# Attention with the values as weights, transposed outputs, and scores from 64-row products of two heads in turn

## The chip, the cores and the metric

The kernel runs on one core of a Trainium2 chip. The core has a matrix engine (TensorE, PE in the profile), which multiplies a stationary operand (the weights, up to 128 rows by 128 columns) with a moving one (up to 512 columns) and writes to PSUM; VectorE (DVE), ScalarE (ACT) and GpSimd (POOL), which work elementwise; SyncE (SP), from whose queue nearly all DMA transfers start; and 16 DMA engines. The metric is the device time of one execution in microseconds (us). Three runs of the kernel before took 1360.21, 1360.32 and 1365.02 us, median 1360.32.

## The reference, cut to what matters

One layer of a hybrid decoder with 1024 tokens of width 1024, in float32: a norm and one projection, then an attention group (8 heads of 64) beside an RWKV-7 group, an output projection with a norm and a residual, and a feed-forward block. The change is in the attention and in the output projection behind it:

```python
A = causal LongNet-style dilated sliding-window attention, branches (128,1),(512,4),(2048,16),
    branch outputs combined by their softmax denominators; then RMSNorm over the attention group
...
attn = _rms_norm(_dilated_attention(q, k, v), attn_out_gain[i])
mixed = jnp.concatenate([attn, rw], axis=-1) @ w_out[i]
x = x + _rms_norm(mixed, norm_mix_post[i])
```

All three branches together are one softmax over all keys up to the query, in which a key counts as often as branches reach it. The kernel therefore adds one strip of constants to the scores (`stripT`, the logarithm of that count, or a very large number where no branch reaches) and does one softmax for each query.

## The kernel before

**Order of the work.** The norm, the projections and the RWKV-7 group come first (lines 194 to 819); there an explicit order for PE and SP is written out. Three projections of the last head pair (`z_aq`, `z_ak`, `z_av`, of which the last two remain) are left over as `rest` and run beside the attention. Then come four calls of `attn_pair(p)` (line 837), one for each pair of heads, at a raised priority, with loads of output weights (`load_wo`, line 923) in between. From there to the end of the attention the order on each engine is chosen when the program is built: a list scheduler takes, by priority and by its own estimate of times, what is ready. Each engine then executes its own list in that order, waiting on semaphores where needed.

**One head pair.** Queries and keys lie in DRAM (`zs_d`) with channels on the partitions: 128 rows, two heads of 64. For each head the query is loaded twice, into both halves of the partitions; the upper half becomes the rounded value (type fp32r, which TensorE multiplies in one pass) and the lower half the remainder, so that one product over 128 rows multiplies both parts of the query with the rounded key (`kh`, also twice) and a second one with the key's remainder (`kl`): two products for each head, `mm` in line 888. Scores have 128 queries on the partitions and up to 1024 keys in the columns, in one or two banks of PSUM (`pS`, tag `w`, two banks). For query block i (0 to 7), both heads: VectorE adds the strip and finds the minimum (line 890; the query is scaled by -0.125, so the largest score is the minimum), ScalarE takes the exponential with its sum in `den` (line 893), PE transposes up to eight blocks of 128 (line 900), and ScalarE (first four) and VectorE (the others) copy them out as `PT` (lines 902, 904).

**The value product.** `av` (line 869) multiplies, in full float32, with PT as the weights (128 keys by 128 queries) and 64 columns of the values as the moving operand. A float32 product runs as two passes, each with its weight load. The output `po` has queries on the partitions; four query blocks and both heads share a bank. The value product of block i is issued after the scores and transposes of block i + 1. After four blocks VectorE divides by the sums (line 912), the result goes to `a_d` in DRAM with tokens as rows, ScalarE squares it and VectorE sums the squares for the norm (lines 917, 918).

**The mix.** For each of eight row blocks of tokens, `half_a` (line 975) loads the attention output, scales it by the norm's root `sa`, transposes it and splits it in a rounded part and a remainder; `half_r` (line 970) does so without scaling for the RWKV-7 output. `half_mm` multiplies both with the output weights, three products for each pair of operands (`mm3`, line 49). R halves of the first two blocks are multiplied early and kept in SBUF (`part`), that of the third is put behind the last value product (`issue_after`, line 1062). `mix_x1` (line 988) forms the post norm, the residual and the next norm; `mix_h2` (line 1018) transposes for the feed-forward block. From line 1078 PE's order is written out again.

## Time and profile before

| | us |
|---|---|
| median of three runs | 1360.32 |
| the profiled execution, time | 1361.23 |
| the profiled execution, span | 1359.4 |
| PE busy | 1307.3 |
| VectorE busy | 914.7 |
| ScalarE busy | 625.0 |
| GpSimd busy | 44.7 |
| first to last start of a score product | 471.5 to 629.0 |
| first to last start of a value product | 478.9 to 637.2 |
| first to last start of a product of the mix with `mxa` | 645.5 to 726.9 |

The span is the time between the first and the last instruction in the trace; the device time holds a little more on both sides. Busy times are sums over the whole span for one engine. In rows of the profile, `L47` is the line of the helper `mm`, so products are told apart by the names of their tiles. `128*64 128x64 f32` is the shape of the weights (rows by columns) and of the moving operand. A float32 product appears as two matrix instructions. The granted clock of TensorE was 0.991 of full speed.

### The profile page before, as it was taken

Reading aid. Unit: us, or ns where it says so; the run is one execution under the profiler, and the core shown is the slowest. Engines: PE = TensorE matmul, PEld = TensorE weight load, DVE = VectorE, ACT = ScalarE, POOL = GpSimd, SP = SyncE. Lnnn points to the kernel's source line nnn. Section 1 sums busy time; section 2 is a strip of 40 time slices with the busy share of each in tenths; the row PEclk is TensorE's granted clock in tenths of the full one; section 3 lists DMA queues with packets and bytes.
Section 4 is the critical chain, followed back from the end, with each engine's and each line's share of the span. In section 5 each row is a group of like instructions: output and inputs, shape, how many; then the busy total and the mean of one; then the engine's idle time right before and its main releaser. Section 6 shows DMA issues by size and latency. Waiting matters only on the chain.

```text
span 1359.4 us, 22401 instructions
## 1 busy us (share of the span) xinstructions
PE 1307.3 (96%) x8784; PEld 1086.4 (80%) x8784; DVE 914.7 (67%) x1647; ACT 625.0 (46%) x1026; POOL 44.7 (3%) x56
## 2 busy tenths in 40 slices
PE   6999999999999999999998999999999999999997
PEld 5777887788777798988887888888887888888885
DVE  7867658531678567655788986677766786445686
ACT  7652324233555367654656444343434344443442
POOL 0000000000000100110000000000000002000110
PEclk9999999899999999999999999999999999999999
DMA  7346746676685656321434344444366995346564
GB/s 255 114 170 163 194 125 179 184 206 204 182 248 145 194 145 181 102 55 38 138 121 139 132 168 152 168 153 150 132 209 217 322 349 172 95 139 200 186 215 157
DMA packets 161193, 231.02 MB, mean 170 GB/s; under 512 B 51680, under 2 KB 88800, under 8 KB 161088
## 3 DMA queue, kind: packets, MB, share of 16 engines
q1 hardware_dynamic: 153024, 208.62, 48.8%
q10 hardware_dynamic: 8064, 20.98, 4.6%
q8 instruction: 69, 1.13, 0.4%
q14 instruction: 36, 0.29, 0.1%
HBM read 156.66 MB, written 72.89 MB: 169 GB/s over the span
## 4 chain that ended last, share of the span: by engine, by line
PE 77%; DVE 11%; DMA 5%; ACT 4%; issue 2%; SPq 0%; POOL 0%; DVEq 0%; ACTq 0%; POOLq 0%
PE X L47 12%; PE dX L47 9%; PE Z L47 6%; PE pm L47 5%; PE dZ L47 5%; PE po L47 5%; PE dY L47 3%; PE z_av L47 3%; PE z_k L47 3%; PE Y L47 3%; PE pS L47 3%; PE z_v L47 3%; PE z_aq L47 2%; PE pT L900 2%; PE z_r L47 2%
## 5 line engine op out<-in xcount | busy, mean ns | idle before, releaser
L47 PE MATMUL dX<-wow,wou 128*128 128x512 f32 x768 | 176.6, 390 | 3.3 <-ACT wow L1106 1.8
L47 PEld LDWEIGHTS dX<-wow,wou 128*128 128x128 f32 x768 | 143.6, 188 | 35.6 <-DVE wow L1107 3.4
L47 PE MATMUL dZ<-wow,wou 128*128 128x512 f32 x384 | 87.4, 389 | 0.0
L47 PEld LDWEIGHTS dZ<-wow,wou 128*128 128x128 f32 x384 | 72.1, 188 | 14.9
L1106 ACT ACTIVATE wow<-wd 128x1024 fp32r<-128x1024 f32 x40 | 42.3, 1059 | 87.1 <-PE dZ L47 29.8
L1107 DVE TENSOR_TENSOR wou<-ur,wou 128x1024 fp32r<-128x1024 f32 x56 | 72.0, 1288 | 10.8 <-ACT wou L1106 10.5
L47 PEld LDWEIGHTS po<-Vt,PT 128*128 128x128 f32 x576 | 72.6, 191 | 4.8 <-ACT PT L902 2.2
L47 PE MATMUL po<-Vt,PT 128*128 128x64 f32 x576 | 74.0, 269 | 0.7 <-ACT PT L902 0.4
L1107 DVE TENSOR_TENSOR wow<-wd,wow 128x1024 fp32r<-128x1024 f32 x40 | 49.9, 1251 | 36.3 <-ACT wow L1106 35.8
L1106 ACT ACTIVATE wou<-ur 128x1024 fp32r<-128x1024 f32 x56 | 58.6, 1049 | 26.2 <-DMA ur<-u_d 18.8
L893 ACT ACTIVATE S<-S,mn 128x128 f32<-128x128 f32 (+7 forms) x64 | 49.4, 774 | 20.8 <-DVE mn L890 20.7
L890 DVE CUSTOM_DVE_ANT_0 S<-pS,stripT 128x512 f32<-128x512 f32 (+3 forms) x64 | 37.4, 590 | 26.1 <-PE pS L47 15.9
L1193 ACT ACTIVATE r<-u 128x512 f32<-128x512 f32 x48 | 30.1, 627 | 48.4 <-DVE u L1191 48.1
L47 PE MATMUL z_aq<-hT,wh_aq 128*128 128x512 f32 x128 | 47.3, 424 | 3.5 <-DVE ev_v L192 3.5
L47 PE MATMUL pm<-WO,mxr 128*128 128x512 f32 x192 | 48.6, 398 | 0.0
L902 ACT ACTIVATE PT<-pT 128x512 f32<-128x512 f32 (+3 forms) x64 | 32.9, 515 | 32.2 <-PE pT L900 30.2
L1107 DVE TENSOR_TENSOR wow<-TK,wow 128x1024 fp32r<-128x1024 f32 x16 | 20.8, 1301 | 38.9 <-ACT wow L1106 38.9
L47 PE MATMUL Z<-HB,wo 128*128 128x512 f32 x192 | 46.1, 389 | 0.0
L47 PE MATMUL pm<-WO,mxa 128*128 128x512 f32 x192 | 45.8, 394 | 0.0
L900 PE MATMUL pT<-cst,S 128*128 128x128 f32 x288 | 44.4, 276 | 1.0 <-DVE rden L910 0.5
L47 PE MATMUL X<-HB,wo 128*128 128x512 f32 x180 | 43.6, 390 | 1.6 <-ACT HB L1029 1.6
L47 PE MATMUL z_k<-hT,wh_k 128*128 128x512 f32 x128 | 43.2, 398 | 1.7 <-DVE z L223 1.4
(388 smaller groups left out, 3102.5 us busy)
## 6 DMA issues: line engine op xcount, KB each, us to landing
ur<-u_d SPq DMA_DIRECT2D x56, 512.0 KB, 4.2
wd<-in_wdown_dram SPq DMA_DIRECT2D x40, 512.0 KB, 3.9
u_d<-S SPq DMA_DIRECT2D x64, 256.0 KB, 2.1
u_d<-u SPq DMA_DIRECT2D x48, 256.0 KB, 2.1
wr_upa<-in_wup_dram SPq DMA_DIRECT2D x16, 512.0 KB, 3.8
wr_upb<-in_wup_dram SPq DMA_DIRECT2D x16, 512.0 KB, 3.8
TK<-in_wdown_dram SPq DMA_DIRECT2D x16, 512.0 KB, 7.3
x<-in_x_dram SPq DMA_DIRECT2D x8, 512.0 KB, 6.0
```

The lines of the kernel that those rows point to most:

```text
L47: return PE.matmul(o, lhsT, rhs, start=start, stop=stop, skip_group_check=True)
L890: V.tensor_tensor_reduce(Sx[:, lo:hi], pS[:, :hi - lo], stripT[:, so:so + hi - lo], 1.0, 3e38 if k == 0 else mn[:, 0:1], OP.add, OP.min, a ...
L893: A.activation(Sx[:, :w], Sx[:, :w], AF.Exp, scale=-1.0, bias=mn[:, nbk - 1:nbk], accum_out=den[:, i, h:h + 1])
L900: PE.transpose(pt[:, j], Sx[:, (4 * k + j) * P:(4 * k + j + 1) * P], ident)
L902: A.activation(PT[:, 0:nb_], pt[:, 0:nb_], AF.Copy)
L1106: A.activation(w[:, 0, 0:n], raw, AF.Copy)
L1107: E.tensor_tensor(w[:, 1, 0:n], raw, w[:, 0, 0:n].bitcast(F32), OP.subtract)
L1193: A.activation(r, src, AF.Relu)
```

## The change

- **Scores.** The pair's queries and keys are loaded once, both heads one below the other, and split by ScalarE (rounded) and VectorE (remainder) into `qh`, `ql`, `kh`, `kl`. A head's score is three products over its own 64 rows (remainder with rounded, rounded with rounded, rounded with remainder). The two heads' products alternate: they use different rows of the array and different PSUM banks.
- **Value product.** The values are the weights (128 keys by 64 channels), PT is the moving operand. Two query blocks form a group, 2g and 2g + 1, side by side in the columns (the later block first), so up to 256 columns move. The output `po` has the head's 64 channels on its half of the partitions and queries in the columns: it comes out transposed. The product of group g is issued within block 2g + 2, that of the last group at the end of the pair.
- **Division.** The reciprocals of the sums have queries on the partitions, the output has them in the columns. So they are stored to DRAM (`rd_d`) and read back as rows over 64 partitions (`rb`), and VectorE multiplies behind the product. `a_d` holds the output transposed.
- **Norm of the attention.** The squares of the four pairs are added up in `sqa`, and eight small products with `bone` (two columns of ones) sum them over the channels. `half_a` has neither scaling nor transposes left. The scale `sa` comes in behind: for the first two blocks at the addition of both halves, for the others the R half is scaled by its inverse beforehand and the result afterwards.
- **Buffers.** The input loads share the staging tiles of the weights (`wr`, three), score tiles are two each of two sizes, the pool `ev2` goes away, its tag `ev` has two tiles and is shared with the outputs. The third R product moves from behind the last value product into the loop of the mix.

```diff
-                    for d in range(2):
-                        nc.sync.dma_start(qr[own[d]], zs_d[12 + p, h * 64:h * 64 + 64, :])
-                G.tensor_scalar(qs, qr, -0.125, 0.0, op0=OP.mult, op1=OP.add)
-                V.scalar_tensor_tensor(qs[64:128], qr[64:128], -0.125, qs[64:128].bitcast(F32), OP.mult, OP.subtract)
...
+            for src, T_, sc in ((12, Q, -0.125), (16, K_, 1.0)):
+                raw = stg.tile([P, S], F32, name=f"{'qk'[src > 12]}r{p}", tag="wr", bufs=3)
+                nc.sync.dma_start(raw, zs_d[src + p])
+                th, tl = (ap_.tile([P, S], F32R, ...) for c_ in "hl")
+                A.activation(th, raw, AF.Copy, scale=sc)
+                V.scalar_tensor_tensor(tl, raw, sc, th.bitcast(F32), OP.mult, OP.subtract)
...
-            def av(po, i, ii, PTs):
-                for h in range(2):
-                    for j in range(i + 1):
-                        last_av[0] = mm(po[:, ii, h], PTs[h][:, j], Vt[:, j, h * 64:h * 64 + 64], j == 0, j == i)
+            def av(g, PTs, rb):
+                po = ps.tile([P, 512], F32, name=f"po{p}_{g}", tag="by"[g % 2], bufs=1)[:, 0:256]
+                for j in [0, 2 * g + 1] + list(range(1, 2 * g + 1)):
+                    n = 128 if j > 2 * g else 256
+                    for h in range(2):
+                        last_av[0] = mm(po[own[h], 0:n], Vt[:, j, h * 64:h * 64 + 64], PTs[h][:, 256 * j:256 * j + n], j == 0, j == 2 * g or g == 0)
+                cols = slice(256 * g, 256 * g + 256)
+                ao = ap_.tile([P, 512], F32, name=f"ao{p}_{g}", tag="ev")[:, 0:256]
+                V.tensor_tensor(ao, po, rb, OP.mult)
+                nc.sync.dma_start(a_d[:, p, cols], ao)
...
-                            for q in range(2):
-                                mm(pS[:, :hi - lo], QS[h][:, i * P:(i + 1) * P], (KH, KL)[q][h][:, lo:hi], q == 0, q == 1)
+                        pS = [ps.tile([P, 512], F32, name=f"pS{p}_{i}_{h}_{k}", tag="w") for h in range(2)]
+                        for q, (a_, b_) in enumerate(((1, 0), (0, 0), (0, 1))):
+                            for h in range(2):
+                                mm(pS[h][:, :hi_ - lo_], Q[a_][own[h], i * P:(i + 1) * P], K_[b_][own[h], lo_:hi_], q == 0, q == 2)
...
-                            if k == 0:
-                                A.activation(PT[:, 0:nb_], pt[:, 0:nb_], AF.Copy)
+                            if k == 0 and (h == 0 or nbk == 2):
+                                A.activation(dst, pt[:, 0:nb_], AF.Copy)
                             else:
-                                V.tensor_copy(PT[:, 4:4 + nb_], pt[:, 0:nb_])
+                                V.tensor_copy(dst, pt[:, 0:nb_])
+                    if i % 2 == 0 and pend:
+                        av(*pend.pop(0))
+                V.reciprocal(rden, den)
+                nc.sync.dma_start(rd_d[p, g].rearrange("h s q -> q h s"), rden)
+                rb = ap_.tile([P, 256], F32, name=f"rb{p}_{g}", tag="rb", bufs=1)
+                for h in range(2):
+                    nc.sync.dma_start(rb[own[h]], rd_d[p, g, h:h + 1].rearrange("o s q -> o (s q)").to_broadcast([64, 256]))
...
+        def half_a(t):
+            m = mp.tile([P, 4, P], F32, name=f"ma{t}", tag="ma")
+            nc.sync.dma_start(m, a_d[:, :, (t ^ 1) * P:(t ^ 1) * P + P])
+            mx = stg.tile([P, 2, 4, P], F32R, name=f"mxa{t}", tag="wl")
+            A.activation(mx[:, 0], m, AF.Copy)
+            V.tensor_tensor(mx[:, 1], m, mx[:, 0].bitcast(F32), OP.subtract)
...
-        with tc.issue_after(last_av[0].ins):
-            half_mm(ORD[2], pms[2], rx.pop(2), 4, True, False)
-        V.tensor_reduce(sa[:, 0, :], sq4.rearrange("q p t -> q t p"), axis=AX.X, op=OP.add)
+        pq = ps.tile([P, 8, 2], F32, name="pq", tag="a", bufs=1)
+        for t in range(8):
+            mm(pq[:, t ^ 1], sqa[:, t * P:(t + 1) * P], bone)
+        V.tensor_reduce(sa[:, 0, :], pq, axis=AX.X, op=OP.add)
```

146 lines of the change are left out of this document (64 added, 82 removed).

## The prediction

> **What bounds the kernel now.** I read the page first, then the busy times by stage, then the chain of waits, and last the instructions around the products one by one. The page (busy time of two engines, and the chain that ended last, by engine) says that TensorE, PE, sets the time:
>
> ```profile
> PE 1307.3 (96%) x8784; PEld 1086.4 (80%) x8784; DVE 914.7 (67%) x1647; ACT 625.0 (46%) x1026; POOL 44.7 (3%) x56
> PE 77%; DVE 11%; DMA 5%; ACT 4%; issue 2%; SPq 0%; POOL 0%; DVEq 0%; ACTq 0%; POOLq 0%
> ```
>
> The change touches the attention and the mix that follows it. The busy time by stage, for the attention from the first query load's use to the last output (462 to 638) and for the mix behind it (638 to 730), has the columns PE, weight loads, VectorE, ScalarE, GpSimd:
>
> ```profile
> 462.30:638.00 175.70, 171.38 (x1231) 152.57 (x1230) 107.33 (x272) 102.01 (x224) 17.29 (x16) 1.00 0.42 117
> 638.00:730.00 92.00, 88.79 (x443) 73.80 (x442) 71.32 (x172) 52.60 (x105) 0.00 (x0) 1.00 0.36 121
> ```
>
> In the attention PE lacks only 4.3 of 175.7 us, while VectorE and ScalarE are busy 107.3 and 102.0. So PE work taken out here comes out of the time, up to the point where the softmax chain on the other two engines sets the pace. The end of the chain of waits for the last head pair, and the same stretch as PE's timeline, show the hand-over:
>
> ```profile
> 637.49 0.70 DVE ao L912
> 638.21 2.15 DMA a_d<-ao
> 640.43 2.58 DMA ma<-a_d
> ```
> ```profile
> 632.87 1.06 PE L900 MATMUL pT<-cst,S 128*128 128x128 f32 x8 [0.48 <-DVE rden L910]
> 633.77 3.68 PE L47 MATMUL po<-Vt,PT 128*128 128x64 f32 x32
> 637.26 5.71 PE L47 MATMUL pm<-WO,mxr 128*128 128x512 f32 x24
> 643.06 0.66 PE L964 MATMUL mxta<-cst,ma 128*128 128x128 f32 x4
> 645.13 0.66 PE L964 MATMUL mxta<-cst,ma 128*128 128x128 f32 x4 [1.41 <-DVE mxa L967]
> 645.54 2.77 PE L47 MATMUL pm<-WO,mxa 128*128 128x512 f32 x11
> ```
>
> The 32 passes of the last value product start 3.49 us before the next group, 0.109 us each; eight transposes take 0.90. While the last output is divided, stored and read back, the third R product (`pm` from `mxr`) covers PE until 643, and PE is whole again at 645.5.
>
> **The value product.** Now there are 288 products in 576 passes (the page's `po` row), weights PT (128 columns), 64 columns moved: 576 x 0.109 = 62.8 us. Afterwards V is the weight (64 columns) and up to 256 query columns move: 40 products a pair, 160 in all, 320 passes, 256 of them 256 columns wide and 64 of them 128. The trace has no such width in full float32; two forms bound it (mean ns of a pass):
>
> ```profile
> L47 PE MATMUL po<-Vt,PT 128*128 128x64 f32 x576 | 74.0, 269 | 0.7 <-ACT PT L902 0.4
> L47 PE MATMUL E<-TR,Zp 64*64 64x128 f32 x256 | 17.4, 275 | 0.0
> L47 PE MATMUL qu<-Z,W 64*64 64x64 f32 x256 | 8.3, 220 | 0.0
> ```
>
> From 64 to 128 columns a pass grows by 55 ns, 0.86 ns a column, so a pass of 256 streams 0.220 us and one of 128 streams 0.110: 56.3 + 7.0 = 63.3 us, exactly what is there now. Everything hangs on whether the two heads, which write different halves of the output partitions, run side by side. The timeline shows such products, `E` (64 weight columns, halves in turn) and `O`, and `p`, which uses the halves of the contracted rows:
>
> ```profile
> 335.56 1.09 PE L47 MATMUL E<-TR,Zp 64*64 64x128 f32 x16
> 336.58 1.15 PE L47 MATMUL O<-VU,TR 128*64 128x64 f32 x32
> 337.67 0.50 PE L47 MATMUL z_aq<-hT,wh_aq 128*128 128x512 f32 x1
> ```
> ```profile
> 283.39 0.40 PE L47 MATMUL z_av<-hT,wh_av 128*128 128x512 f32 x1
> 283.71 1.16 PE L47 MATMUL p<-AR,K 64*128 64x128 f32 x16
> 284.81 0.50 PE L47 MATMUL z_av<-hT,wh_av 128*128 128x512 f32 x1
> 285.14 0.40 PE L47 MATMUL z_av<-hT,wl_av 128*128 128x512 f32 x1
> ```
>
> `E` puts 16 passes of 128 columns into 1.02 us, 0.064 each where 0.110 stream: two at a time, with one slot lost since a head's two passes follow each other (nine slots of 0.110 are 0.99). So I take the halved end of the bounds 31.7 to 63.3, plus one slot of 0.220 for each of the 16 blocks: 35.2 us. The part is worth 62.8 - 35.2 = -27.6 (0 at the other end).
>
> **The scores.** Columns of one product over a pair's eight query blocks, one head: 128 x (1 + ... + 8) = 4608, nine times 512. Two neighbours give the price:
>
> ```profile
> 493.67 0.48 PE L47 MATMUL pS<-kh,qs 128*128 128x512 f32 x1
> 493.99 0.40 PE L47 MATMUL pS<-kl,qs 128*128 128x512 f32 x1
> 494.22 0.60 PE L900 MATMUL pT<-cst,S 128*128 128x128 f32 x4
> ```
>
> A product of 512 takes 0.23 (493.99 to 494.22). Now 4 a pair (two heads, two products): 16 x 9 x 0.23 = 33.1 us. Afterwards 6 a pair, 64 rows each, heads in turn: 49.7 one after another, 24.8 side by side. `p` is the nearest row and is two at a time, though in full float32 and not in the fp32r of the scores: I take 24.8, -8.3, with +16.6 as the other end. One doubt is kept inside: the two heads' banks are freed one behind the other by VectorE, and products issued as each bank comes free stand alone. The second halves of wide blocks are 10 of 36 parts; if half of them run unpaired, that is +3.5.
>
> **Changing the shape of the array.** Around `p`, the step in is 0.32 (283.39 to 283.71) where 0.23 is usual, the step out leaves 1.10 - 0.99 = 0.11, and the next product takes 0.33 to its successor (284.81 to 285.14), 0.10 more: 0.30 in all. Of that 0.09 is paid today wherever fp32r follows float32 (493.67 to 493.99 is 0.32). So 0.2 new for each block. There are 48 score blocks and 16 value blocks: +12.8 us (0 if blocks merge, double if the order splits them). [...]
>
> PE's sum in the attention: -27.6 - 8.3 + 3.5 + 12.8 = -19.6.
>
> **The softmax chain.** Score tiles were three in rotation; now two tiles of each of two sizes serve both heads, so a head's next block of the same size is written only when the transposes have read this one. Its rows (VectorE, first and second half; ScalarE's exponential and its sum; the copy of the transposes):
>
> ```profile
> L890 DVE CUSTOM_DVE_ANT_0 S<-pS,stripT 128x512 f32<-128x512 f32 x40 | 27.6, 690 | 16.2 <-PE pS L47 9.2 <-PE pT L900 5.1 <-ACT S L893 1.7
> L890 DVE CUSTOM_DVE_ANT_0 S<-pS,stripT,mn 128x512 f32<-128x512 f32 x8 | 6.0, 749 | 1.1 <-PE pS L47 0.7
> L893 ACT ACTIVATE S<-S,mn 128x1024 f32<-128x1024 f32 x8 | 9.2, 1149 | 9.3 <-DVE mn L890 9.3
> L893 ACT ACTIVATION_READ_ACCUMULATOR S<-S,mn 128x1 f32 x64 | 12.2, 191 | 0.0
> L902 ACT ACTIVATE PT<-pT 128x512 f32<-128x512 f32 x40 | 23.8, 594 | 29.2 <-PE pT L900 27.4 <-PE pS L47 1.8
> ```
>
> For the widest block: 0.69 + three products 0.69 + 0.75 + two exponentials 2 x 1.34 (ScalarE takes both heads before it can copy) + 0.59 + transposes 0.90 = 6.3 us. PE's work for that block today is 8 x 0.23 + 16 x 0.11 + 32 x 0.109 = 7.1. So a pair can shrink to some 0.89 of today's 35 us of PE work (33.1 + 62.8 + 31.7 for 288 transposes, a quarter, with 3 for V's transposes and changes of type): 31, while PE's new sum is 35 - 4.9 = 30. That costs 1 to 2 a pair where no other work fills PE; pair 0 has the last projections, pairs 1 and 2 have two R products. I add +4 (0 to +10).
>
> **Inputs, copies and division.** The 32 half loads of queries and keys become eight whole ones. GpSimd's 16 roundings go to ScalarE, eight of 1.06; VectorE's 16 differences become eight of 1.22:
>
> ```profile
> L854 DVE TENSOR_TENSOR kl<-kr,kh 128x1024 fp32r<-128x1024 f32 x8 | 9.8, 1220 | 5.0 <-POOL kh L122 4.9
> L1106 ACT ACTIVATE wow<-wd 128x1024 fp32r<-128x1024 f32 x40 | 42.3, 1059 | 87.1 <-PE dZ L47 29.8
> ```
>
> Sixteen narrow copies (blocks 0 to 3, second head) move from ScalarE to VectorE, the eight reductions become twelve half-width additions. Each engine stays near 100 us, under PE's 156: nothing in the sum. Without PE's cover the new split would stand as 1.06 + 1.22 before each pair; the next pair's tiles are double, so it lies under the pair before.
>
> The quotients now make a round trip: the reciprocals are stored as single numbers and read back over 64 partitions. Nothing like it is in the trace; small and plain transfers bound it (KB, us to landing):
>
> ```profile
> z_d<-Zt SPq DMA_DIRECT2D x4, 128.0 KB, 4.0
> a_d<-ao SPq DMA_DIRECT2D x8, 256.0 KB, 2.3
> ma<-a_d SPq DMA_DIRECT2D x8, 256.0 KB, 2.7
> ```
>
> 2.3 + 2.7 = 5.0 at the low end, twice 4.0 = 8.0 at the high end. The value product comes a block later, so the cover is the next block: by PE's sum for a block as above, 7.1 for the widest and less in proportion to its width, it is 6.2 us for block 6 and 4.4 for block 4, but 2.7 for block 2; the last group has its own product, 3.5. On SP's queue the reads wait for the store; behind them stand the next output's store and the next pair's loads, each needed a block or a pair later. I take 0 here; the rival below takes the rest.
>
> **The mix.** Attention outputs come transposed, so 32 transposes go (645.13 to 645.54: four in 0.41): -3.3. Eight small products of squares come, 16 passes; the nearest row is
>
> ```profile
> L47 PE MATMUL pst<-cst,sq 128*128 128x2 f32 x64 | 7.4, 246 | 0.0
> ```
>
> 7.4 / 64 = 0.116: +1.9. Scaling of eight A halves (now unscaled) becomes scaling of six R halves, the same count less two; two one-column operations are added to each of six row blocks on VectorE, under the products of the next block. The third R product no longer covers the hand-over, but the A halves need neither scale nor transposes, so the first two A products (48 passes of 0.23, 11 us) can stand there instead, while squares, sum and root are formed. Nothing in the sum: -1.4 for the part.
>
> **Sum.** -19.6 + 4 - 1.4 = -17.0. The profiled execution took 1361.2 (span 1359.4), 0.9 above the median of the runs, so 1360.3 - 17.0 = 1343.
>
> **Rivals.** (a) PE's saving arrives whole: pairs never part (-3.5), the chain never binds (-4), and idle time of today goes too: 1331 to 1336. For it speaks that PE had filling work in three of the four pairs; against it, the waits of both other engines on mn and pT, and their load.
> (b) The 64-row products in fp32r do not run side by side: 16.6 + 8.3 - 3.5 = 21.4 more, 1364. Only `p`, in float32, speaks against it. If the value product doesn't pair either, the change doesn't do what it says: another 28, 1392; `E` and `O` speak against that plainly.
> (c) Slower, by the round trip of the reciprocals: VectorE works in order, and the division of a group stands ahead of the next block's scores. In the first and the last group of each pair the cover is 2.7 to 3.5 us against 5 to 8. It decides from 17 / 8 = 2.1 us of stall in each of these eight groups; at 3.5 it is +28, 1371. [...]
>
> **How the numbers follow.** Forecast 0.45 (1336 to 1352 by its own terms), (a) 0.20, (b) 0.12 and 0.05, (c) 0.15, 0.03 for others. About 0.5%, 6.8 us, is what a measurement of this kernel can tell from no change. Faster takes the forecast and (a): 0.66 with a little off for the forecast's upper end and a little on for a mild (c). Same is mostly (b): 0.13. Slower is (c) and the double failure: 0.21. The range runs from below (a) to short of a full (c): 1327 to 1368.
>
> **What would show it.** Value passes start at about 0.11 us on average with both heads alternating; six score products of 512 take about 0.7, not 1.4; shape changes cost 0.3 around a block; PE idle in the attention stays under 10 us. VectorE waiting for `rb` at the division would show (c). The prediction is wrong if products of one head stand alone in the timeline, or if pairs last as long as today with PE idle.

## The result: 8% slower

The changed kernel takes 1475.03 us (median of four runs, 1474.62 to 1482.21), the kernel before beside it 1362.61: a ratio of 1.0837, 95% interval 1.0795 to 1.088. The forecast was 1343, its range ended at 1368, and no rival reached that far. The page of the changed kernel (busy times, the granted clock in 40 slices, the chain that ended last by engine and by line):

```profile
PE 1364.4 (93%) x8608; PEld 1073.7 (73%) x8608; DVE 913.8 (62%) x1689; ACT 629.4 (43%) x1024; POOL 27.4 (2%) x40
...
PEclk9999999999998688888789999999999999999998
...
PE 64%; DMA 18%; DVE 11%; ACT 3%; issue 3%; SPq 1%; DVEq 0%; ACTq 0%
PE X L47 11%; PE dX L47 8%; DMA rd_d<-rden 7%; PE Z L47 6%; PE pm L47 5%; PE dZ L47 4%; DMA rb<-rd_d 4%; PE dY L47 3%; PE z_ak L47 3%; PE z_k L47 3%; PE Y L47 3%; PE z_v L47 2%; PE z_av L47 2%; PE z_aq L47 2%; DMA wd<-in_wdown_dram 2%
```

Before, DMA had 5% of the chain and PE 77%. Now 18% is DMA, of which the two legs of the reciprocals' round trip (`rd_d`, `rb`) take 11% of the span, and the clock line, which was 9 nearly throughout, shows 6 to 8 in the slices of the attention. By stage (attention, and the mix behind it; columns as in the prediction):

```profile
467.40:747.50 280.10, 229.87 (x1091) 142.00 (x1092) 107.40 (x303) 109.37 (x227) 0.00 (x0) 0.81 0.30 68
747.50:842.50 95.00, 86.75 (x413) 71.67 (x411) 72.58 (x183) 50.20 (x101) 0.00 (x0) 0.96 0.34 112
```

From the first score product to the last value product it was 165.7 us (471.5 to 637.2) and is 279.3 (467.4 to 746.7): all of the loss lies here. The mix took 92.6 from there to the feed-forward block and takes 95.8. PE lacked 4.3 us of the attention, now it lacks 50, at a clock of 0.81. The groups of PE and of the division, and the two transfers (KB, us to landing):

```profile
L904 PE MATMUL pT<-cst,S 128*128 128x128 f32 x288 | 55.1, 325 | 13.2 <-ACT S L897 7.6 <-ACT sqa L870 3.9 <-DVE PT L910 1.1
L47 PE MATMUL po<-PT,Vt 128*64 128x256 f32 (+1 forms) x320 | 53.9, 424 | 1.5 <-ACT Vt L856 1.0 <-DVE ao L867 0.5
L47 PE MATMUL pS<-kh,ql 64*128 64x512 f32 (+3 forms) x96 | 40.4, 506 | 27.0 <-DVE mn L893 24.0 <-DVE ql L847 2.8
```
```profile
L867 DVE TENSOR_TENSOR ao<-po,rb 128x256 f32<-128x256 f32 x16 | 6.8, 424 | 67.7 <-DMA rb<-rd_d 56.6
```
```profile
rb<-rd_d SPq DMA_DIRECT2D x32, 64.0 KB, 4.2
rd_d<-rden SPq DMA_DIRECT2D x16, 2.0 KB, 9.8
```

The division stands idle 67.7 us on VectorE, 56.6 of it for `rb`. A store of 2 KB takes 9.8 us to land: it writes 512 single numbers to 512 places. The pages of the changed kernel and of the kernel without the trip (run 1 below) differ by 8960 packets of under 512 bytes (60384 and 51424):

```profile
DMA packets 171945, 228.95 MB, mean 155 GB/s; under 512 B 60384, under 2 KB 101600, under 8 KB 171840
```
```profile
DMA packets 160937, 226.82 MB, mean 162 GB/s; under 512 B 51424, under 2 KB 90592, under 8 KB 160832
```

How such a wait spreads, from the timeline at the end of one pair:

```profile
652.67 0.66 PE L904 MATMUL pT<-cst,S 128*128 128x128 f32 x4
652.77 3.98 SPq L918 DMA_DIRECT2D rb<-rd_d  x2
659.00 0.42 DVE L867 TENSOR_TENSOR ao<-po,rb 128x256 f32<-128x256 f32 x1 [7.11 <-DMA rb<-rd_d]
659.48 0.90 PE L855 MATMUL vt<-cst,vT 128*128 128x128 f32 x3 [6.16 <-DVE ao L867]
```

VectorE waits 7.11 us for the reciprocals, the bank of the output isn't free, and PE, whose next work in order needs that bank, stands still for 6.16.

For what follows I added up PE's time from the start of each product to the start of the next, by tile, from 460 us to the first product of the feed-forward block; in brackets the waits in it (idle time over 30 ns). It is worked out from the instructions of each trace, in us:

```
                     before       changed      run 1        run 9        run 17
                                  (all of it)  (no trip)    (values      (values alone,
                                                            alone)       whole blocks)
scores pS            46.7 ( 3.0)  95.4 (22.7)  69.5 ( 2.7)  56.1 ( 7.2)  64.9 (13.8)
transposes pT        29.6 ( 0.0)  55.9 ( 7.3)  45.3 ( 1.2)  37.5 ( 3.8)  37.1 ( 6.2)
value product po     60.9 ( 0.6)  56.0 ( 4.7)  45.9 ( 0.4)  49.8 ( 2.4)  37.3 ( 0.0)
projections z_a*     22.3 ( 0.5)  37.9 ( 3.3)  37.3 ( 3.9)  32.5 ( 7.9)  32.0 ( 7.9)
mix pm               90.7 ( 0.2) 119.6 (21.5)  94.0 ( 1.3)  94.8 ( 2.9)  96.8 ( 4.7)
all                 269.7 ( 7.5) 382.4 (61.3) 307.6 (11.2) 288.6 (26.1) 285.1 (34.4)
```

"All" has the small tiles too. The projections' row depends on how many of them fall behind 460; the other rows do the same task in every column, the scores as three 64-row products in the second and third.

### The profile page after: what moved, and what is told of

It is laid out like the page before. It is cut to its first block, busy times and chain, and to the rows that moved or that the text cites. A ratio compares the mean times of both kernels' runs of the same rounds, so it can differ in the third digit from the quotient of the medians.

```text
span 1473.3 us, 22106 instructions
## 1 busy us (share of the span) xinstructions
PE 1364.4 (93%) x8608; PEld 1073.7 (73%) x8608; DVE 913.8 (62%) x1689; ACT 629.4 (43%) x1024; POOL 27.4 (2%) x40
## 2 busy tenths in 40 slices
DMA packets 171945, 228.95 MB, mean 155 GB/s; under 512 B 60384, under 2 KB 101600, under 8 KB 171840
## 4 chain that ended last, share of the span: by engine, by line
PE 64%; DMA 18%; DVE 11%; ACT 3%; issue 3%; SPq 1%; DVEq 0%; ACTq 0%
PE X L47 11%; PE dX L47 8%; DMA rd_d<-rden 7%; PE Z L47 6%; PE pm L47 5%; PE dZ L47 4%; DMA rb<-rd_d 4%; PE dY L47 3%; PE z_ak L47 3%; PE z_k L47 3%; PE Y L47 3%; PE z_v L47 2%; PE z_av L47 2%; PE z_aq L47 2%; DMA wd<-in_wdown_dram 2%
## 5 line engine op out<-in xcount | busy, mean ns | idle before, releaser
L904 PE MATMUL pT<-cst,S 128*128 128x128 f32 x288 | 55.1, 325 | 13.2 <-ACT S L897 7.6
L47 PE MATMUL pS<-kh,ql 64*128 64x512 f32 (+3 forms) x96 | 40.4, 506 | 27.0 <-DVE mn L893 24.0
L904 PEld LDWEIGHTS pT<-cst,S 128*128 128x128 f32 x288 | 38.6, 164 | 34.6 <-ACT S L897 11.5
L910 DVE COPY PT<-pT 128x128 f32<-128x128 f32 (+3 forms) x48 | 23.5, 490 | 55.7 <-PE pT L904 55.6
L47 PE MATMUL po<-PT,Vt 128*64 128x256 f32 (+1 forms) x320 | 53.9, 424 | 1.5 <-ACT Vt L856 1.0
L47 PEld LDWEIGHTS pS<-kh,ql 64*128 64x128 f32 x96 | 17.1, 210 | 51.2 <-DVE mn L893 34.2
L47 PE MATMUL pm<-WO,mxr 128*128 128x512 f32 x192 | 53.4, 421 | 0.0
L47 PE MATMUL z_ak<-hT,wh_ak 128*128 128x512 f32 x128 | 49.7, 442 | 0.0
L47 PE MATMUL pm<-WO,mxa 128*128 128x512 f32 x192 | 48.9, 408 | 0.0
L867 DVE TENSOR_TENSOR ao<-po,rb 128x256 f32<-128x256 f32 x16 | 6.8, 424 | 67.7 <-DMA rb<-rd_d 56.6
L893 DVE CUSTOM_DVE_ANT_0 S<-pS,stripT 128x512 f32<-128x512 f32 (+3 forms) x64 | 36.7, 584 | 17.7 <-PE pS L47 8.6
```

Of the source, the lines that this page charges most:

```text
L47: return PE.matmul(o, lhsT, rhs, start=start, stop=stop, skip_group_check=True)
L867: V.tensor_tensor(ao, po, rb, OP.mult)
L893: V.tensor_tensor_reduce(Sx[h][:, lo_:hi_], pS[h][:, :hi_ - lo_], stripT[:, so:so + hi_ - lo_], 1.0, 3e38 if k == 0 else mn[h][:, 0:1], OP ...
L904: PE.transpose(pt[:, j], Sx[h][:, (4 * k + j) * P:(4 * k + j + 1) * P], ident)
L910: V.tensor_copy(dst, pt[:, 0:nb_])
```

## The experiments

Eighteen kernels ran, in five sets, each set beside the kernel before on the same chip (medians there 1361.1 to 1362.7). They are told in the order in which the questions came up.

**1 to 4. How much is the round trip?** Run 1 leaves it out, and the division with it (the divisor is a tile of ones).

```diff
-                nc.sync.dma_start(rd_d[p, g].rearrange("h s q -> q h s"), rden)
-                rb = ap_.tile([P, 256], F32, name=f"rb{p}_{g}", tag="rb", bufs=1)
-                for h in range(2):
-                    nc.sync.dma_start(rb[own[h]], rd_d[p, g, h:h + 1]...to_broadcast([64, 256]))
+                rb = one
```

> The changed kernel with the round trip of the reciprocals taken out and nothing in its place: the outputs are multiplied by a tile of ones, so the division by the sums of the softmax is left out. Theory T (the trip makes VectorE wait at the division, and TensorE's clock falls because it is starved): about 1345 us (1335 to 1358), no wait of the division for a transfer, granted clock at 0.98 or above. Rival R1 (the 64-row products, alone and with their changes of shape, and the low clock that they cause, make the loss): above 1400 us, clock near 0.95 as in the changed kernel. Rival R2 (any trip through DRAM of this kind costs it, whatever its size) says the same as T here.

Measured: 1396.78 us, ratio 1.0228 (1.0174 to 1.0281). The trip and what hangs on it cost 78 us of the 113; but 35 stay, where theory T had 1335 to 1358. (The four times of run 1 go from 1388 to 1402, so its differences are good to some 7 us.) Run 2 keeps the trip and mends the store: PE transposes the reciprocals first, so that four rows of 512 bytes are written.

```diff
+                PE.transpose(pof[0:4, 256:384], rden.rearrange("p h s -> p (h s)"), ident)
+                V.tensor_copy(rr, pof[0:4, 256:384])
-                nc.sync.dma_start(rd_d[p, g].rearrange("h s q -> q h s"), rden)
+                nc.sync.dma_start(rd_d[p, g].rearrange("h s q -> (h s) q"), rr)
```

> The changed kernel with the reciprocals transposed on TensorE first, so that the store writes four rows of 512 B in place of 512 single numbers; the trip itself stays. Theory T in its narrow form (the 512 single numbers of the store make the trip long): the store lands in about 2.5 us in place of 9.8, the trip takes about 7 in place of 14, and at least half of the 113 us comes back: 1380 to 1415. R2: under 40 us come back, above 1435. R1: above 1440 too, with the clock unchanged near 0.95.

Measured: 1405.77, ratio 1.0329 (1.0285 to 1.0373). The wait for `rb` (waits of the whole run: us, times, longest) is

```profile
DVE ao L867 <- DMA rb<-rd_d: 7.6, 3, 5.5
```

7.6 us in place of 56.6. With the division kept, 69 of the 78 us come back: nearly all of the trip's price was the 512 small writes, not the trip. Run 3 does without DMA: GpSimd spreads the reciprocals on a diagonal (`ident` x `rden`), PE multiplies it with ones into the free half of the output's bank.

```diff
+                        G.tensor_scalar(dg[:, h, s_], ident, rden[:, h, s_:s_ + 1], None, op0=OP.mult)
...
+                        mm(pof[own[h], 256 + 128 * s_:384 + 128 * s_], one, dg[:, h, s_])
+                A.activation(rb, pof[:, 256:512], AF.Copy)
```

> The changed kernel with the whole function but no trip: GpSimd multiplies the identity by the reciprocals, a product with 64 columns of ones spreads them over the output's partitions in the free half of the output's PSUM bank, ScalarE copies them out. T: as without the trip, plus 64 short products (7 us at most when paired) and 16 copies: 1345 to 1365. R1: above 1400.

Measured: 1404.65, ratio 1.0315 (1.0276 to 1.0353). Three kernels without the slow store, all 35 to 44 us above the kernel before. Run 4 puts the scores of before (128 rows, two products) into run 3.

```diff
-                        for q, (a_, b_) in enumerate(((1, 0), (0, 0), (0, 1))):
-                            for h in range(2):
+                        for h in range(2):
+                            for q in range(2):
+                                mm(pS[h]..., QS[h][...], (KH, KL)[q][h][:, lo_:hi_], q == 0, q == 1)
```

> As the one with the reciprocals spread by TensorE, but the scores as in the kernel before: two products over 128 rows for each head, queries and keys loaded twice. It shows the value product and the transposed outputs alone. T with the prediction's prices: the scores lose 8.3 us of saving but 48 blocks lose their 0.2 us for a change of shape, so within 8 us of the version with 64-row scores, 1340 to 1365. R1: at least 30 us below the version with 64-row scores.

Measured: 1398.82, ratio 1.0263 (1.0231 to 1.0294). The 64-row scores aren't the rest of the loss; here they cost 5.8 us.

**5 to 8. Order, staging, or the value product?** In run 1 PE's timeline between 645 and 650.4 us shows what the list scheduler makes of the blocks:

```profile
644.95 0.39 PE L47 MATMUL pS<-kh,qh 64*128 64x512 f32 x1
645.18 0.39 PE L47 MATMUL pS<-kl,qh 64*128 64x512 f32 x1
645.51 0.49 PE L47 MATMUL pm<-WO,mxr 128*128 128x512 f32 x1
645.93 0.32 PE L47 MATMUL pS<-kh,ql 64*128 64x128 f32 x1
646.10 0.27 PE L47 MATMUL pS<-kh,qh 64*128 64x128 f32 x1
646.21 0.27 PE L47 MATMUL pS<-kl,qh 64*128 64x128 f32 x1
646.41 0.66 PE L906 MATMUL pT<-cst,S 128*128 128x128 f32 x4
646.99 0.33 PE L47 MATMUL pS<-kh,ql 64*128 64x128 f32 x1
...
648.74 0.87 PE L47 MATMUL po<-PT,Vt 128*64 128x256 f32 x8
649.54 0.33 PE L906 MATMUL pT<-cst,S 128*128 128x128 f32 x1
649.80 0.65 PE L47 MATMUL po<-PT,Vt 128*64 128x256 f32 x4
```

Three products of one head alone (128 columns, 0.48 us with the way out), four transposes, then the other head; a value product cut by a single transpose. From 460 us to the feed-forward block the array changes its shape 219 times in run 1 (207 in the changed kernel; one into and one out of each of the prediction's 64 blocks make 128), and the 16 value products lie in 44 pieces. Run 5 chains the six score products of a block so that the heads alternate; run 6 gives the raw queries, keys and values of the first pair two score tiles in place of the weights' staging tiles; run 7 does both.

```diff
+                              with (tc.issue_after(last_s[0].ins) if q or h else nullcontext()):
+                                last_s[0] = mm(pS[h]...
...
-                raw = stg.tile([P, S], F32, ..., tag="wr", bufs=3)
+                raw = ap_.tile([P, S], F32, ..., tag="S2") if p == 0 else stg.tile(...)
```

> The kernel without the round trip (reciprocals spread on PE, 1404.65), with the six score products of a block put into one fixed order, so that the two heads alternate and no product of one head stands alone. Theory 'order' (what is left over 1362 comes from products of one head that run alone and from broken-up blocks): pS busy time in the attention falls from some 72 us to under 50, and the time falls by 15 to 25 us, to 1380 to 1390. Theory 'staging' (the raw tiles of pair 0 share three staging tiles with the weights of the projections; PE loses pace before the attention and the clock is low at its start): within 6 us of 1404.65, the clock still at 0.5 to 0.7 at 470 to 500 us. Theory 'rows' (64-row products in fp32r do not run side by side at all): within 6 us of 1404.65, and six products of 512 take some 1.4 us although the heads alternate.

> The kernel without the round trip (1404.65), with the raw queries, keys and values of pair 0 in two of the attention's own score tiles in place of the staging tiles of the weights. Theory 'staging': the projections before the attention run as before (PE busy about 18.4 of each 20 us from 360 to 440), the clock is back at 0.9 or more from 470 us on, and the time falls by 15 us or more, to under 1390. Theories 'order' and 'rows': within 6 us of 1404.65.

> Both of the two edits before: pair 0's raw tiles out of the staging tiles, and the six score products in one fixed order. If 'order' and 'staging' each hold a part and add up, 1360 to 1375; if only one holds, the better of the two kernels before within 6 us; if 'rows' holds, over 1390.

Measured: 1412.93 (ratio 1.0372, 1.034 to 1.0405), 1406.82 (1.0334, 1.0308 to 1.036) and 1407.64 (1.0334, 1.0312 to 1.0356), against 1404.65: none gains. Staging is out. A chain alone lets other work in between its links; it didn't make the blocks whole. Run 8 asks for the value product alone, with the scores and the raw tiles of before.

> The kernel without the round trip, with the scores as they were before (128-row products, two a block, raw tiles of their own as before): the value product, its transposed outputs and the mix stand alone. If the value product is worth what was forecast (-27.6, with 16 changes of shape +3 and the spreading of the reciprocals about +5), 1335 to 1350, and the scores and their staging account for all that is left. If the value product is itself a cause of the loss (it doesn't pair, or the clock falls under it), 1375 or more. If it merely gains nothing, 1358 to 1366.

Measured: 1399.15 (1.0295, 1.0252 to 1.0338). So the value product with all that comes with it here (transposed outputs, reciprocals spread on PE, shared tiles) costs 38 us where 27.6 had been forecast as its gain. Which of these costs it, this run doesn't show.

**9 to 12. Whole blocks by force, values without reciprocals, projections first.** Run 9 is run 1 with the scores of before (value product, transposed outputs and mix alone, nothing divided).

> The kernel without the division (divisor a tile of ones), with the scores and their raw tiles as they were in the kernel before: the value product with the values as weights, transposed outputs and the mix stand alone, with no reciprocal work on any engine. If the value product is worth what was forecast (-27.6, +3 for changes of shape, -1.4 in the mix), 1335 to 1345. If the order breaks its 16 blocks into 50 and more pieces, 1350 to 1375. If it loses for another reason that has nothing to do with the scores or the reciprocals, over 1380, as with the reciprocals spread on PE (1399.15).

Measured: 1379.11 (1.0124, 1.0095 to 1.0154). Between 1375 and 1380 nothing had been written down; it is 17.7 us below run 1, which is the price of the 64-row scores with their loads there (8.3 had been forecast as a gain; between runs 3 and 4 it was 5.8), and 17.6 above the kernel before. In run 10 each group of score products and each value product is one section that nothing is put into; run 11 puts the last projections ahead of the first pair; run 12 does both.

```diff
+                with tc.tile_critical():
                     (the products of a block)
...
+        for _ in rest:
+            pass
         for p in range(3):
```

> The kernel without the division (1396.78; divisor a tile of ones), with the six score products of a half block and all passes of a value product each issued as one section that nothing is put into, so that the heads always alternate and no block is broken up. The time is that of PE's order and pairing. Theory 'order' (the loss left after the round trip is broken-up blocks, lone products and the changes of shape that they bring): pieces of the value product fall from 41-44 to 16, PE's time in value passes from 46 to about 36 us and in score products from 70 to under 50, changes of shape from 219 to some 130, and the kernel takes 1360 to 1380. Theory 'clock' (PE stands idle ahead of the first products and the clock then stays at 0.5 for tens of us): the clock is as low from 467 to 500 us as before, and the time stays within 8 us of 1396.78. Each section adds an empty instruction and a branch on PE; if these cost 0.3 us or more each, 64 and more of them hide a gain, and the timeline shows it.

> The kernel without the division (1396.78), with the last projections (a quarter of the key and value projections, some 20 us of PE) put ahead of the first pair instead of under it. Theory 'clock': the first pair's inputs are ready when PE comes to them, PE doesn't stand idle, the clock stays at 0.9 or more from 460 to 520 us, and 10 to 18 us are gained: 1379 to 1387. Theory 'order': no gain, 1390 to 1405, since the first pair loses its filling work.

> Both: whole blocks and the last projections first, without the division. If 'order' and 'clock' each hold a part, 1345 to 1368; if 'order' alone, 1360 to 1380; if 'clock' alone, 1379 to 1387; if neither, about 1397.

Measured: 1547.21, 1417.3 and 1562.68. PE's queue drains in each of the 48 sections of the scores (row of the line that opens them; ns, shortest, middle and longest):

```profile
L892 PEldq DRAIN  x48: 387/854/1505, 473.4 to 802.4; - x48
```

So these times say nothing on order. But the blocks of run 10, in a stretch at full clock, settle what a whole block takes:

```profile
583.60 0.50 PE L47 MATMUL pS<-kh,ql 64*128 64x512 f32 x2 [1.03 <-DVE rden L918]
583.93 0.40 PE L47 MATMUL pS<-kh,qh 64*128 64x512 f32 x2
584.17 0.39 PE L47 MATMUL pS<-kl,qh 64*128 64x512 f32 x2
584.64 0.50 PE L47 MATMUL z_ak<-hT,wh_ak 128*128 128x512 f32 x1
...
591.64 1.73 PE L47 MATMUL po<-PT,Vt 128*64 128x256 f32 x16 [0.55 <-ACT S L901]
593.46 0.49 PE L47 MATMUL z_av<-hT,wl_av 128*128 128x512 f32 x1
```

A pair of 512-column products on 64 rows starts 0.24 after the pair before it (583.93 to 584.17), the time of one product alone (0.23): the two do run side by side in fp32r. Six take 1.04 with the way in and out (583.60 to 584.64); before, the same block took four of 0.23. Sixteen value passes take 1.82. Projections first (run 11) lose 20 us: the first score product starts at 485.9 in place of 466.7 in run 1, and the attention behind it is no shorter (211.4 and 212.9). What the projections take ahead of it isn't won back; both theories had missed this.

**13 to 16. The shared tiles of the last projections.** In runs 1 to 10 and in the changed kernel PE stands idle ahead of the first pair. The change also let the outputs share the tiles (`ev`, two) into which the last projections leave their banks. Run 16 puts only that into the kernel before, where the projections had three such tiles and the outputs one of their own. Run 13 gives the outputs a tile of their own in run 1, run 14 in the changed kernel, run 15 in run 9; the projections keep two.

```diff
-                ao = ap_.tile([P, 512], F32, name=f"ao{p}_{g}", tag="ev")[:, 0:256]
+                ao = ap_.tile([P, 256], F32, name=f"ao{p}_{g}", tag="ao", bufs=1)
```

> The kernel before with only this part of the change: the last projections are taken out into two tiles of the attention's pool, which the outputs share; nothing else is touched. Theory 'banks': PE loses its filling work under the first pair here too, 1372 to 1390. Theory 'order' alone: 1358 to 1366, no change.

> The kernel without the division (1396.78), with one edit more: the outputs get a tile of their own, and the two tiles that take the last projections out of their banks are no longer shared with them (the divisor is one column of ones). Theory 'banks' (because of the shared tiles the projections' banks are emptied only after four outputs of the first pair, at 524 to 548 us in place of 460; PE then has nothing to put under the softmax chain, stands idle ahead of the first pair and its clock falls): all four key and value halves leave their banks before 530 us, PE is busy over 19 of 20 us from 460 to 480 and the clock is at 0.9 or more from 480 us on; 1360 to 1378. Theory 'order' alone (lone products, broken blocks, some 220 changes of shape): within 6 us of 1396.78.

> The changed kernel (1475) with that one edit alone: outputs in a tile of their own (the scratch of the squares makes room), all else as changed, the round trip too. Theory 'banks': 20 to 35 us less, 1440 to 1455. Theory 'order' alone: within 8 us of 1475.

> The value product alone, without the division (1379.11, scores as before), with the outputs in a tile of their own. Theory 'banks': PE's idle time ahead of the first pair goes, and the kernel takes 1345 to 1362, below the kernel before. Theory 'order' alone: within 6 us of 1379.

Measured: 1384.42 (1.0148, 1.0114 to 1.0182) for the kernel before with shared tiles: +22 us from two shared buffers in place of four. The stores of the last projections, in the kernel before and then in this one (first and last issue), and PE's stage there:

```profile
L699 ACTq DMA_DIRECT2D zs_d<-ev_aq x8: 326/330/355, 254.3 to 460.1; - x8
L699 ACTq DMA_DIRECT2D zs_d<-ev_ak x8: 326/326/353, 271.1 to 470.2; - x8
```
```profile
L700 ACTq DMA_DIRECT2D zs_d<-ev_aq x8: 326/326/397, 256.0 to 516.3; - x8
L700 ACTq DMA_DIRECT2D zs_d<-ev_ak x8: 326/327/350, 272.9 to 555.1; - x8
```
```profile
460.00:480.00 20.00, 10.54 (x44) 8.27 (x43) 9.48 (x15) 4.96 (x9) 4.23 (x4) 0.83 0.77 214
```

The last query half leaves its bank at 516 in place of 460. The first pair's first output (written at 493, stored by 496) comes ahead of it in the two tiles; until then the projections' banks stay occupied, no projection starts from 467.6 to 517.9, and PE is busy 10.54 of 20 us. Undoing it in the changed kernels gives 1404.79 (run 13, ratio 1.0319, 1.0246 to 1.0392), 1470.09 (run 14, 1.0771, 1.0735 to 1.0807) and 1391.04 (run 15, 1.0202, 1.0167 to 1.0237): 5 us less with the trip, nothing in the other two, although the last query half leaves its bank at 469 and 466 us there (542 and 524 in runs 1 and 9), and PE is busy throughout from 460 to 480 in run 15. So the stall moves and isn't cured. Runs 13 and 15 also carry 8 to 9 us in the feed-forward block that have another cause (last section), so what the edit is worth there isn't shown.

**17 and 18. Whole value products without sections.** In run 17 the first product of a block is the one whose operand comes last, and the block's products go ahead of all else that is ready. In PE's list, which is fixed when the program is built, that makes 16 pieces of 49 and 31 changes of shape of 97.

```diff
-                for j in [0, 2 * g + 1] + list(range(1, 2 * g + 1)):
+                with tc.high_priority(offset=100000):
+                  for k, j in enumerate([2 * g, 2 * g + 1] + list(range(2 * g))):
...
-                    for h in range(2):
+                    for h in (1, 0):
```

> The value product alone without the division (1379.11, scores as before), with one edit: a block's first product is the one whose operand comes last, and the products of a block go ahead of everything else that is ready, so each of the 16 blocks stands whole in PE's order (16 pieces in place of 49, 31 changes of shape in place of 97); no section, no branch. Theory 'order' (the value product's gain went into broken-up blocks): value passes take some 37 us of PE in place of 50, transposes and scores 5 to 10 us less, and 15 to 25 us are gained: 1354 to 1364. Theory 'chain' (the softmax chain, or the late banks, set the pace in this form of the kernel whatever PE has to do): PE's idle time grows by what its work shrinks, and the time stays within 6 us of 1379.

Measured: 1377.48 (1.0111, 1.0084 to 1.0138), 1.6 us below run 9, which the noise doesn't tell from nothing. The groups of the value product in run 9 and in run 17, and then PE's longest waits in run 17 from 460 us to the feed-forward block (us, times, longest):

```profile
L47 PE MATMUL po<-PT,Vt 128*64 128x256 f32 (+1 forms) x320 | 50.8, 381 | 1.3 <-ACT PT L921 0.5 <-DVE ao L880 0.3 <-ACT Vt L869 0.2
```
```profile
L47 PE MATMUL po<-PT,Vt 128*64 128x256 f32 (+1 forms) x320 | 38.5, 392 | 2.9 <-DVE PT L924 2.1 <-DVE ao L881 0.5
```
```profile
PE pT L918 <- ACT S L911: 8.9, 9, 3.1
PE pS L47 <- POOL kh L124: 7.0, 1, 7.0
PE pS L47 <- DVE mn L907: 4.9, 8, 0.9
```

The value passes shrink from 49.8 to 37.3 us (table above; the columns "values alone" and "values whole" are runs 9 and 17), and PE's waits grow from 26.1 to 34.4, while scores and products of the mix take longer around them. Of these waits 13.8 us are for exponentials and minima (0.5 in the kernel before) and 7.0 are one wait for the first pair's keys. That is what theory "chain" had said of the time, the softmax chain or the late banks: most of what PE no longer does, it waits. The granted clock, 0.94 from 460 to 655, is a rival for part of it: an estimate from it, 0.06 of 195 us, is 12 at most. Run 18 is all of the reference: the kernel before with this value product, whole blocks, the store of run 2, outputs in a tile of their own, and the softmax of before head by head.

> All of the reference: the kernel before with the value product alone changed (values as weights, transposed outputs, the changed mix), whole blocks as in the run beside it, the reciprocals transposed on PE and sent round as four rows of 512 bytes, outputs in a tile of their own, and the softmax of before (one head at a time, three score tiles of full width). If whole blocks and the softmax of before bring the forecast gain of the value product: -27.6 + 5 (changes of shape) + 2 (transposes of reciprocals) - 1.4 (mix) = 1340 to 1348. If the chain takes half of it, 1350 to 1357. If a group of two blocks needs more cover than the pair gives (theory 'chain'), 1362 or more.

Measured: 1380.8 (1.0132, 1.0107 to 1.0157). Waits of PE there: 11.3 us for exponentials, the longest 4.8. From the first score product to the last value product it takes 168.4 us (477.1 to 645.5) where the kernel before takes 165.7. No version beats the kernel before. But of the 15.6 us between the two profiled executions (1375.0 and 1359.4) only 2.7 lie in the attention; 5.6 lie ahead of the first score product and 8.3 in the feed-forward block, products of unchanged work being slower in both places (last section), and the mix takes 1.0 less. Counted as in the table, the value passes take 38.4 us, PE's waits 24.1 and all 277.0: 22.5 us of value work are gone, and the time from 460 us to the feed-forward block is 7.3 longer. Against run 17 the attention is 14 us shorter, although the trip is back. Several edits lie between the two; the outputs' own tile gained nothing in run 15, which makes the softmax of before the likelier one; it wasn't tested alone.

## Why the prediction was wrong, point by point

- **The round trip, "5.0 to 8.0", "I take 0 here".** This is the step that failed first and cost most: a term put at 0 that measured 78 of the 113 us. The mechanism of rival (c) was right, and it decided; place and size were off. The bounds came from stores of whole rows (2.3 and 4.0 us); a store of single numbers took 9.8 and the loads 4.2. And 11 of the 16 groups waited for `rb`, up to 10.7 us, where 8 were forecast at 3.5. Rival (c) had +28; run 1 gives 78 with the lost clock in it.
- **"PE work taken out here comes out of the time, up to the point where the softmax chain sets the pace."** This step failed too, and it fails even with the trip mended. The part was priced at +4 (0 to +10). Run 17 shows the value product at 37.3 us, as forecast (35.2 plus part of the changes of shape), and it isn't in the time: PE's waits are 34.4 instead of 7.5. I had compared the chain for one block (6.3 us) with PE's work for one block and saw a near tie; I took the other pairs' filling work as given, but a near tie of averages leaves waits at single blocks (17 for exponentials and minima in run 17). PE at 171.4 of 175.7 us didn't show that PE was the only limit. That the kernel before was already balanced is argued, not shown: every run that took value work out also regrouped the blocks.
- **"48 score blocks and 16 value blocks", "0.2 new for each block", "double if the order splits them".** The price of a change was right: in run 1's timeline a 512-column product takes 0.23 to the next of its kind (644.95 to 645.18) and 0.33 to one of another shape (645.18 to 645.51), and the way in took 0.42 (645.51 to 645.93). The number was wrong: 207 changes in place of 128 (two for each block), since the list scheduler breaks blocks. In the kernel before it does so too (its timeline has scores in 87 pieces and values in 80), but there all shapes are alike, so a break is no change of shape.
- **The scores, 24.8 us side by side.** Rival (b) is out: they do pair. But whole they take 1.04 where the old block took 0.92, and in the kernel heads run alone: 69.5 us in run 1. The doubt of 3.5 us for the second halves of wide blocks should have covered all halves: the prediction's own reason, that VectorE frees the two heads' banks one after the other, holds in each block. That this is what makes the lone products is argued, not shown.
- **"Inputs, copies and division: nothing in the sum."** The shared tiles stood in the diff and in my own account of it, and I gave them no line. Alone they cost 22 us (run 16).
- **What held:** values pair two heads (16 passes in 1.82); from the start of the last value product to the feed-forward block run 17 takes 90.1 us (655.1 to 745.2) and run 1 88.0, against 92.6: -2.5 and -4.6 where -1.4 was forecast for the mix. The small products of squares took 1.72 in runs 1, 9 and 17 (1.9 forecast; 2.24 in the changed kernel).
- **Not in the prediction at all: the clock** (last section).

By difference along runs 1 and 9: 78 us trip and its store, 18 the 64-row scores, 17 the value product in its groups of two with the shared tiles. The parts depend on the order in which they are taken out: between runs 3 and 4 the scores are 6. How the last 17 divide is open: shared tiles cost 22 alone, yet undoing them gained nothing with the values turned, and in run 18, with the softmax of before as well, the attention is 2.7 us longer than in the kernel before. The clock's share in the 113 isn't shown, since no run held the clock up; from the granted clock (0.81 over 280.1 us, 0.96 over 95.0) an estimate is 57 us at most.

## What to carry to other kernels

When an engine is busy 97% of a stage, take out its work only after a look at what would end its waits next: here two other engines at 60%, in a chain block by block, were enough to turn a shorter product (49.8 to 37.3 us) into a longer wait (26.1 to 34.4). Look at every tile that a change lets two streams share, and ask which bank stays occupied while one waits for the other. Store single numbers through a transpose (69 of 78 us here), and price changes of shape by the order that PE's list really has (207 here in place of 128).

## What the runs showed of the hardware

**The clock stayed low with the engine busy.** In the kernel before, the granted clock is 1.00 from 460 to 740. In run 1 PE waits 3.6 us for the first pair's queries (last column of its group), and then (windows of 16 us):

```profile
L47 PE MATMUL pS<-kh,ql 64*128 64x512 f32 (+3 forms) x96 | 38.1, 469 | 5.4 <-DVE ql L849 3.6 <-DVE mn L895 1.6
```
```profile
468.00:484.00 16.00, 16.00 (x39) 8.47 (x40) 6.60 (x19) 6.16 (x17) 0.00 (x0) 0.50 0.50 163
484.00:500.00 16.00, 16.00 (x54) 9.16 (x52) 7.35 (x18) 6.87 (x13) 0.00 (x0) 0.50 0.22 74
500.00:516.00 16.00, 15.77 (x86) 9.25 (x84) 7.41 (x24) 7.61 (x14) 0.00 (x0) 0.96 0.03 10
```

32 us with PE busy throughout, at half the clock. The products are slower there: one of `z_ak` takes 0.42 us to the next (468.81 to 469.23) where 0.22 is taken before (462.54 to 462.76). In the changed kernel such a stretch took 23.9 us (from 468.8), in run 2 some 20, in run 13, with 64-row scores too, some 10, in runs 9 and 17, with the scores of before, some 14, in part idle (the runs worked out from windows of 4 us). In runs 3 and 6 the clock was 0.71 and 0.83 from 460 to 480 and 0.77 and 0.58 from 480 to 500. So a wait of 2.8 us (the changed kernel) or 3.6 (run 1) ahead of the first pair was followed by 24 to 32 us at half the clock; that the wait brought the low clock about isn't shown.

In these traces neither the fall nor the return goes by the idle time alone. In the kernel before the clock fell at 92.2 us, where PE had been busy 11.88 of the 12 us from 80 to 92. In the changed kernel it was low from 404.0 for 3.4 us behind a wait of 2.58 us, and from 468.8 for 23.9 behind one of 2.79, seven times as long, with PE busy 3.00 of 3 us from 404 and 23.70 of 23.8 from 468.4. Why it varies so is open: run 13 has the 64-row products of run 1 and was back in 10 us.

**Products of 512 columns at 394 ns in place of 389.** In runs 13, 15 and 18, and in none of the others, products of unchanged work are slower, such as these of the feed-forward block (run 1 and run 13, weights and inputs the same):

```profile
L47 PE MATMUL dZ<-wow,wou x384: 389/389/389, 1213.5 to 1343.9; 128*128 128x512 f32 x192
```
```profile
L47 PE MATMUL dZ<-wow,wou x384: 393/395/397, 1217.2 to 1351.3; 128*128 128x512 f32 x192
```

From the block's first product to the end these three take 638 to 642 us, the kernel before 629.6 and run 1 632.6: some 8 us that have nothing to do with the attention. The projections ahead of the attention are slower in run 18 too (`z_aq`: 232 ns from one start to the next, 18 from 459.87 to 464.04, and 227 in the kernel before, 15 from 454.84 to 458.24). What the three share is another size of the pool of small tiles (a column of four bytes more in runs 13 and 15; in run 18 a tile of 512 bytes more and two of 64 less), which moves every tile behind it. The traces point to the address of the moving operand, without settling it: in run 13 `pm<-WO,mxr` and `X<-HB`, whose operand lies in pools at the other end of SBUF (`side="right"` in the code), take 389 ns in the middle, as `X<-HB` does in run 1, while `X<-T3h`, whose operand lies behind the small tiles, takes 393 (389 in run 1). In run 15 the products of the R half go 228 ns from one start to the next (23 from 678.54 to 683.78), those of the A half 233 (12 from 675.74 to 678.54). Against it stands `X<-T3l`, with its operand at the other end: 392 in runs 13 and 15, 388 in run 18, 389 in run 1. The R and A half of the mix in run 13 (operand at the other end, operand behind the small tiles; ns, shortest, middle and longest), and the A half in run 1:

```profile
L47 PE MATMUL pm<-WO,mxr x192: 387/389/774, 621.6 to 755.0; 128*128 128x512 f32 x192
L47 PE MATMUL pm<-WO,mxa x192: 389/396/484, 675.6 to 761.5; 128*128 128x512 f32 x192
```
```profile
L47 PE MATMUL pm<-WO,mxa x192: 387/389/499, 670.7 to 764.7; 128*128 128x512 f32 x192
```

No run moved a tile on purpose, so whether it is the address, and why, stays open.
